# Token sums on VectorE behind the fourth plain tile, a fourth raw-weight buffer, and block results formed in place, in a chain of four transformer layers

## The chip, the cores and the metric

The kernel runs on one core of one Trainium2 chip. The metric is the device time of one execution, in microseconds (us). A core has five engines that run their own instruction queues in order: TensorE (PE) for matmuls, VectorE (DVE), ScalarE (ACT) and GpSimd (POOL) for elementwise work, and SyncE (SP), which here issues the DMA loads of the weights. Semaphores join them.

## The reference

The input is 512 tokens of 1024 features in float32. Two hybrid layers (retention, sparse and dilated attention, then an MLP) and a norm are followed by two layers with a mixer and a gated feed-forward part each. What the change touches is the MLP and the gated part, cut to this:

```python
# hybrid layer, twice: w_up is 1024 x 4096, w_down 4096 x 1024
h = rms_norm(x, mlp_norm_w)
x = x + jnp.square(jax.nn.relu(h @ w_up)) @ w_down

# second block, two layers: w_gate and w_up are 1024 x 2816, w_down 2816 x 1024
h = rmsnorm(x, ffn_pre_g[layer])
x = x + rmsnorm((jax.nn.silu(h @ w_gate) * (h @ w_up)) @ w_down, ffn_post_g[layer])
```

## The kernel before

**Layout.** Activations lie feature-major: x is eight tiles of 128 features by 512 tokens. Each float32 operand of a matmul is split into a high half (rounded to the matmul's type, on ACT) and a low half (the rest, on DVE or POOL), and a product is three matmuls (mm3, L318 to L323: high by high, high by low, low by high). A weight tile is loaded by SP into `raw` (three buffers, L255), its high half goes into `whi` (L268) and its low half into `wlo` (L269), three buffers each. A plain output tile is 8 x 3 matmuls of 512 columns.

**Pairs.** Most output tiles of the up and gate projections are made two at a time by `seven` (L402): two tiles by two halves of the tokens, each with two halves of the 1024 inputs, are a 2 x 2 block product, done with seven block products instead of eight (Winograd's form of Strassen's scheme). It needs sums of blocks of the weights and sums of blocks of the tokens. `pair_weights` (L374) loads the two raw tiles and forms a1 (a plain half), s12 and s34 (the weight sums, with four POOL operations, L393 to L397, in two buffers of the tag "sum", then split into `shi` and `slo`, L386 and L387) and a2. `token_sums` (L352) forms the token sums once a stage: for each of four feature blocks k, two scaled tiles on ACT (L359), four differences of 128 x 256 on POOL (L363 to L366, into a buffer of "sum"), a high half on ACT (L369) and a low half on DVE (L370).

**A pair's steps.** `seven` is a generator with three steps. The first runs products p1, p2 and p3 (12 matmuls of 256 columns each), copies p1 to r1 (L426) and adds it to p2 (r2, L427). The second runs p1 with the other plain half and p2 with s34; r3 is formed (L433) and one half of u (L434). The third runs p2 with a2 and p3 with s34 and forms the last halves (L438, L439); `post` then does the activation and the split (low half on POOL, L276). `pairs` runs steps one of this pair, three of the pair before, two of this pair, so two pairs are open at once. The tiles t and u come from the tag "t" (four buffers, `temp`, L235), from which `squared`, `tile` and `token_sums` take theirs too.

**Order.** A scheduler sets each engine's order when the kernel is built: it works through instructions by program order as they become ready in its own timing, and gives buffers of a tag to the takers in program order. `after` adds an edge that holds an instruction behind another one without a semaphore where both are on one engine. In the hybrid layers' `mlp` the program has three plain up tiles, `token_sums`, the fourth plain tile, then pairs (L991 to L994); there `post` and `squared` need two squares and the low half of a square on POOL for each tile. In the feed-forward `swiglu` it has three plain tiles, `token_sums`, and the fourth plain tile inside the second call of `product` (L1393 to L1396). `token_sums` runs four times in all, `seven` 64 times: 13 pairs in each hybrid MLP and 19 in each feed-forward stage.

## Time and profile before

| what | value |
|---|---|
| median of 3 runs | 2594.86 us (2590.73 to 2604.97) |
| the profiled execution's own time | 2592.7 us |
| its span | 2590.8 us |
| mean granted TensorE clock | 0.969 of full speed |
| busy share PE, DVE, ACT, POOL | 92%, 66%, 47%, 41% |
| DMA | 215.70 MB, 83 GB/s in the mean |

The span runs from the first to the last instruction of the profiled execution. Times of rows are microseconds from the span's start unless a row says ns. PEclk is the granted clock of PE as a share of its full 2.4 GHz. In a timeline row a bracket holds how long the engine stood idle before the instruction and what ended that wait.

### The profile page before, as it was taken

Reading aid. Unit: us, or ns where it says so; the run is one execution under the profiler, and the core shown is the slowest. Engines: PE = TensorE matmul, PEld = TensorE weight load, DVE = VectorE, ACT = ScalarE, POOL = GpSimd, SP = SyncE. Lnnn points to the kernel's source line nnn. Section 1 sums busy time; section 2 is a strip of 40 time slices with the busy share of each in tenths; the row PEclk is TensorE's granted clock in tenths of the full one; section 3 lists DMA queues with packets and bytes.
Section 4 is the critical chain, followed back from the end, with each engine's and each line's share of the span. In section 5 each row is a group of like instructions: output and inputs, shape, how many; then the busy total and the mean of one; then the engine's idle time right before and its main releaser. Section 6 shows DMA issues by size and latency. Waiting matters only on the chain.

```text
span 2590.8 us, 35121 instructions
## 1 busy us (share of the span) xinstructions
PE 2375.4 (92%) x13521; PEld 2040.4 (79%) x13521; DVE 1702.5 (66%) x2713; ACT 1216.1 (47%) x1945; POOL 1062.8 (41%) x755
## 2 busy tenths in 40 slices
PE   9899969999998997999998996999899987799997
PEld 7787868898877876888887874888886765788886
DVE  6978644554488875554558677756757675857655
ACT  5566553443365665343343564443434554444332
POOL 3464363342145644343312435543521543724531
PEclk9999989999999998999999998999999999899998
DMA  5211213333232211333332211333232321232322
GB/s 166 90 62 46 78 58 97 98 99 97 91 102 78 62 53 45 106 92 96 98 98 78 74 57 33 92 96 92 85 97 71 97 80 43 78 100 86 96 90 74
DMA packets 63848, 215.70 MB, mean 83 GB/s; under 512 B 7104, under 2 KB 7232, under 8 KB 63680
## 3 DMA queue, kind: packets, MB, share of 16 engines
q1 hardware_dynamic: 62064, 207.06, 26.1%
q0 software_dynamic: 1472, 6.29, 0.7%
q8 instruction: 106, 1.74, 0.3%
q14 instruction: 62, 0.51, 0.1%
q10 hardware_dynamic: 144, 0.11, 0.0%
HBM read 211.33 MB, written 2.10 MB: 82 GB/s over the span
## 4 chain that ended last, share of the span: by engine, by line
PE 63%; DVE 21%; ACT 5%; POOL 5%; issue 5%; DMA 1%; POOLq 0%; ACTq 0%; DVEq 0%; SPq 0%
PE mm L323 18%; PE mm L322 17%; PE mm L321 17%; DVE wlo L387 2%; PE st L322 2%; PE st L321 2%; PE st L323 2%; DVE slo L387 1%; DVE t L1367 1%; DVE x L1067 1%; ACT shi L386 1%; DMA raw<-in_w1up 1%; DVE score L739 1%; DVE t L1366 1%; PE st L307 1%
## 5 line engine op out<-in xcount | busy, mean ns | idle before, releaser
L268 ACT ACTIVATE whi<-raw 128x1024 fp32r<-128x1024 f32 (+2 forms) x286 | 277.8, 973 | 536.9 <-PE mm L322 361.3
L321 PE MATMUL mm<-xg,whi 128*128 128x512 f32 (+1 forms) x1280 | 448.1, 356 | 80.3 <-ACT r L426 34.2
L321 PE MATMUL mm<-act,whi 128*128 128x512 f32 x1160 | 456.8, 396 | 13.2 <-ACT act L275 8.3
L323 PE MATMUL mm<-xg,wlo 128*128 128x512 f32 (+1 forms) x1280 | 453.7, 355 | 11.1 <-DVE wlo L387 7.8
L322 PE MATMUL mm<-act,whi 128*128 128x512 f32 x1160 | 460.7, 397 | 0.8 <-POOL act L276 0.8
L323 PE MATMUL mm<-act,wlo 128*128 128x512 f32 x1160 | 461.1, 398 | 0.0
L322 PE MATMUL mm<-xg,whi 128*128 128x512 f32 (+1 forms) x1280 | 454.1, 355 | 0.2 <-DVE xg L315 0.2
L269 POOL TENSOR_TENSOR wlo<-raw,whi 128x1024 fp32r<-128x1024 f32 (+3 forms) x109 | 257.8, 2367 | 297.8 <-ACT whi L268 277.0
L321 PEld LDWEIGHTS mm<-xg,whi 128*128 128x128 f32 x1280 | 244.3, 192 | 121.3 <-ACT r L426 34.9
L387 DVE TENSOR_TENSOR slo<-sum,shi 128x1024 fp32r<-128x1024 f32 x128 | 176.2, 1377 | 229.9 <-ACT shi L386 220.4
L276 POOL TENSOR_TENSOR act<-t,act 128x512 fp32r<-128x512 f32 x108 | 160.5, 1495 | 346.3 <-ACT act L275 346.2
L323 PEld LDWEIGHTS mm<-xg,wlo 128*128 128x128 f32 x1280 | 244.6, 191 | 45.9 <-DVE wlo L387 8.8
L322 PEld LDWEIGHTS mm<-xg,whi 128*128 128x128 f32 x1280 | 245.2, 192 | 38.1 <-DVE xg L315 6.6
L321 PEld LDWEIGHTS mm<-act,whi 128*128 128x128 f32 x1160 | 221.0, 191 | 65.7 <-ACT act L275 11.1
L386 ACT ACTIVATE shi<-sum 128x1024 fp32r<-128x1024 f32 x128 | 135.8, 1061 | 272.3 <-POOL sum L394 169.5
L322 PEld LDWEIGHTS mm<-act,whi 128*128 128x128 f32 x1160 | 218.8, 189 | 52.8 <-DVE act L276 2.3
L323 PEld LDWEIGHTS mm<-act,wlo 128*128 128x128 f32 x1160 | 218.6, 188 | 47.8
L269 DVE TENSOR_TENSOR wlo<-raw,whi 128x1024 fp32r<-128x1024 f32 (+3 forms) x177 | 201.6, 1139 | 76.5 <-ACT whi L268 75.7
L393 POOL TENSOR_TENSOR sum<-raw 128x512 f32<-128x512 f32 x64 | 86.4, 1350 | 389.1 <-DMA raw<-in_w1up 179.4
L323 PE MATMUL mm<-tok,slo 128*128 128x256 f32 x512 | 150.6, 294 | 38.9 <-DVE slo L387 38.9
L387 DVE TENSOR_TENSOR wlo<-raw,whi 128x1024 fp32r<-128x1024 f32 (+1 forms) x128 | 153.6, 1202 | 9.3 <-ACT whi L386 9.3
L321 PE MATMUL mm<-tok,shi 128*128 128x256 f32 x512 | 148.6, 290 | 9.4 <-DVE r L427 6.8
(275 smaller groups left out, 5241.5 us busy)
## 6 DMA issues: line engine op xcount, KB each, us to landing
raw<-in_w1up SPq DMA_DIRECT2D x64, 512.0 KB, 3.6
raw<-in_w1down SPq DMA_DIRECT2D x64, 512.0 KB, 3.6
raw<-in_gate SPq DMA_DIRECT2D x44, 512.0 KB, 3.7
raw<-in_up SPq DMA_DIRECT2D x44, 512.0 KB, 3.6
raw<-in_w1fm SPq DMA_DIRECT2D x41, 512.0 KB, 3.5
raw<-in_down SPq DMA_DIRECT2D x48, 384.0 KB, 3.1
raw<-in_odin SPq DMA_DIRECT2D x16, 512.0 KB, 3.7
raw<-in_w1out SPq DMA_DIRECT2D x16, 384.0 KB, 3.0
```

The lines of the kernel that those rows point to most:

```text
L268: nc.scalar.activation(hi[:, sl], raw[:, sl], AF.Copy)
L269: (low or nc.gpsimd).tensor_sub(lo[:, sl], raw[:, sl], hi[:, sl].bitcast(F))
L276: (low or nc.vector).tensor_sub(lo, t, hi.bitcast(F))
L307: mm(ps, a[:, rows], b[hh][:, cols], start=True, stop=False, skip_group_check=True)
L321: mm(ps, w[0], a[0], start=first, stop=False, skip_group_check=True)
L322: mm(ps, w[0], a[1], start=False, stop=False, skip_group_check=True)
L323: self.last_mm = mm(ps, w[1], a[0], start=False, stop=last, skip_group_check=True)
L386: nc.scalar.activation(hi[:, :width], t, AF.Copy)
L387: nc.vector.tensor_sub(lo[:, :width], t, hi[:, :width].bitcast(F))
L393: nc.gpsimd.tensor_add(s1, a21, a22)
L739: nc.vector.match_replace(sl, m8, sl, TAKEN)
L1067: add = eng.tensor_add(self.x[c], self.x[c], m[c])
```

## The change

Five edits. (1) The `raw` tag gets four buffers, not three. (2) In `token_sums` the first scaled tile of a block comes from a tag "b1" of its own with one buffer, the second from "t" as before; the four differences go from POOL to DVE. (3) The high half of each token sum is ordered on ACT behind the last plain tile's weight high half that was issued before the call (`last_high`). (4) The fourth plain tile comes ahead of `token_sums` in both stages. (5) In `seven` the buffer r is 256 wide, not 768: r2 is formed in the half of t, and r3 in the half of u, in which the result will stand, so t and u are taken in the first step.

```diff
--- before.py
+++ after.py
@@ -185,7 +185,7 @@
         zero = self.cp.tile([128, 128], R, name="zero")
         nc.vector.memset(zero.bitcast(F), 0.0)
         self.keep_warm(14, of=zero)
-        self.early = [self.wp.tile([128, 1056], F, tag="raw", name=self.name("raw")) for _ in range(3)]
+        self.early = [self.wp.tile([128, 1056], F, tag="raw", name=self.name("raw"), bufs=4) for _ in range(3)]
         for c in range(8):
             nc.sync.dma_start(self.x[c], I["x"][c * 128:(c + 1) * 128, :])
             if c in (0, 3):
@@ -253,7 +253,7 @@
 
 
     def load(self, src, width):
-        raw = self.wp.tile([128, 1056], F, tag="raw", name=self.name("raw"))
+        raw = self.wp.tile([128, 1056], F, tag="raw", name=self.name("raw"), bufs=4)
         self.nc.sync.dma_start(raw[:, :width], src)
         return raw
 
@@ -265,7 +265,7 @@
         lo = self.wp.tile([128, 1056], R, tag="wlo", name=self.name("wlo"))
         for a in range(0, width, step):
             sl = slice(a, a + step)
-            nc.scalar.activation(hi[:, sl], raw[:, sl], AF.Copy)
+            self.last_high = nc.scalar.activation(hi[:, sl], raw[:, sl], AF.Copy)
             (low or nc.gpsimd).tensor_sub(lo[:, sl], raw[:, sl], hi[:, sl].bitcast(F))
         return hi, lo
 
@@ -352,21 +352,21 @@
     def token_sums(self, x, g):
 
 
-        nc, out = self.nc, []
+        nc, out, high = self.nc, [], self.last_high
         for k in range(4):
-            b = [self.temp() for _ in range(2)]
-            for i in range(2):
-                nc.scalar.activation(b[i], x[k + 4 * i], AF.Copy, scale=g(k + 4 * i))
-            (b11, b12), (b21, b22) = [(t[:, :256], t[:, 256:]) for t in b]
+            b1, b2 = self.temp("b1", 1), self.temp()
+            for i, b in enumerate((b1, b2)):
+                nc.scalar.activation(b, x[k + 4 * i], AF.Copy, scale=g(k + 4 * i))
+            (b11, b12), (b21, b22) = [(b[:, :256], b[:, 256:]) for b in (b1, b2)]
             f = self.get("sum", 2 * S)
             t1, t2, t3, t4 = [f[:, 256 * i:256 * i + 256] for i in range(4)]
-            nc.gpsimd.tensor_sub(t1, b12, b11)
-            nc.gpsimd.tensor_sub(t2, b22, t1)
-            nc.gpsimd.tensor_sub(t3, b22, b12)
-            nc.gpsimd.tensor_sub(t4, b21, t2)
+            nc.vector.tensor_sub(t1, b12, b11)
+            nc.vector.tensor_sub(t2, b22, t1)
+            nc.vector.tensor_sub(t3, b22, b12)
+            nc.vector.tensor_sub(t4, b21, t2)
             t = self.get("tok", 4 * S, R)
             hi, lo = t[:, :2 * S], t[:, 2 * S:]
-            nc.scalar.activation(hi, f, AF.Copy)
+            self.after(nc.scalar.activation(hi, f, AF.Copy), high)
             nc.vector.tensor_sub(lo, f, hi.bitcast(F))
             out.append((hi, lo))
         return out
@@ -418,25 +418,23 @@
                 self.mm3(ps, (w[0][:, sl], w[1][:, sl]), b(k), first and k == 0, k == 3)
 
         p1, p2, p3 = (t[:, :256] for t in (self.mm_tile(), self.mm_tile(), self.st_tile()))
-        r = self.get("r", 768)
-        r1, r2, r3 = (r[:, 256 * i:256 * i + 256] for i in range(3))
+        r, t, u = self.get("r", 256), self.temp(), self.temp()
         product(p1, a1, 0, plain(0, 0), True)
         product(p2, s12, 1, summed(1), True)
         product(p3, s12, 0, summed(0), True)
-        nc.scalar.activation(r1, p1, AF.Copy)
-        nc.vector.tensor_add(r2, p2, r1)
+        nc.scalar.activation(r, p1, AF.Copy)
+        nc.vector.tensor_add(t[:, half[1]], p2, r)
         yield
-        t, u = self.temp(), self.temp()
         product(p1, a1, 1, plain(1, 0), False)
         product(p2, s34, 0, summed(2), False)
         nc.scalar.activation(t[:, half[0]], p1, AF.Copy)
-        nc.vector.tensor_add(r3, p2, r1)
-        nc.vector.tensor_add(u[:, half[1]], p3, r3)
+        nc.vector.tensor_add(u[:, half[1]], p2, r)
+        nc.vector.tensor_add(u[:, half[1]], p3, u[:, half[1]])
         yield
         product(p2, a2, 0, summed(3), False)
         product(p3, s34, 1, plain(1, 1), False)
-        nc.vector.tensor_add(u[:, half[0]], p2, r1)
-        nc.vector.tensor_add(t[:, half[1]], p3, r2)
+        nc.vector.tensor_add(u[:, half[0]], p2, r)
+        nc.vector.tensor_add(t[:, half[1]], p3, t[:, half[1]])
         post(t, u)
         yield
 
@@ -989,8 +987,8 @@
                 next(left.pop())
 
         up(range(3))
+        up([3])
         tok = self.token_sums(x, lambda c: self.v("mlp_norm", 8 * l + c))
-        up([3])
         pairs([4, 6])
         for g in range(4):
             if g < 3:
@@ -1391,9 +1389,10 @@
                 nc.vector.tensor_add(m[j], m[j], ps)
 
         p = self.fm_tiles([plain("gate", 0), plain("up", 0), plain("gate", 1)], xg)
+        last = self.fm_tiles([plain("up", 1)], xg)[0]
         tok = self.token_sums(self.x, lambda c: self.v("ffn_pre", 8 * l + c))
         product(0, tile(p[0]), tile(p[1]))
-        product(1, tile(p[2]), tile(self.fm_tiles([plain("up", 1)], xg)[0]))
+        product(1, tile(p[2]), tile(last))
         pairs(range(2, 6))
         for g, n in enumerate((6, 6, 6, 4)):
             if g < 3:
```

## Rows read from the trace of the kernel before

**Rows 1.** The page's busy table: engine, busy us, share of the span, instructions.

```profile
PE 2375.4 (92%) x13521; PEld 2040.4 (79%) x13521; DVE 1702.5 (66%) x2713; ACT 1216.1 (47%) x1945; POOL 1062.8 (41%) x755
```

**Rows 2.** Busy time by stretch, inside the first wait: engines, granted clock, DMA share, GB/s.

```profile
342.00:352.00 10.00, 0.00 (x0) 0.00 (x0) 3.60 (x4) 5.63 (x8) 8.28 (x10) 0.50 0.00 0
```

**Rows 3.** PE's timeline (start, us, operation, idle before) and waits (total, times, longest).

```profile
352.57 0.58 PE L321 MATMUL mm<-xg,whi 128*128 128x256 f32 x1 [17.03 <-ACT r L426]
355.27 0.58 PE L321 MATMUL mm<-tok,shi 128*128 128x256 f32 x1 [0.20 <-ACT shi L386]
362.68 0.35 PE L321 MATMUL mm<-tok,shi 128*128 128x256 f32 x1 [2.52 <-DVE r L427]
...
1608.76 0.80 PE L321 MATMUL mm<-xg,whi 128*128 128x512 f32 x1 [16.02 <-ACT whi L268]
...
POOL sum L393 <- DMA raw<-in_w1up: 179.4, 19, 17.4
...
PE mm L323 <- DVE slo L387: 38.9, 26, 2.4
PE mm L321 <- ACT r L426: 34.2, 3, 17.0
PE mm L321 <- ACT whi L268: 32.6, 3, 16.0
```

**Rows 4.** Timelines of ACT and POOL in the first hybrid MLP, around the token sums.

```profile
350.67 1.06 ACT L369 ACTIVATE tok<-sum 128x1024 fp32r<-128x1024 f32 x1 [2.77 <-POOL sum L366]
...
352.15 0.36 ACT L426 ACTIVATE r<-mm 128x256 f32<-128x256 f32 x1
...
331.93 3.91 POOL L276 TENSOR_TENSOR act<-t,act 128x512 fp32r<-128x512 f32 x3
...
350.60 1.26 POOL L393 TENSOR_TENSOR sum<-raw 128x512 f32<-128x512 f32 x1
```

**Rows 5.** Durations by line: ns min/median/max, first and last start us, forms.

```profile
L359 ACT ACTIVATE t<-x,vec_sb x32: 705/707/726, 330.4 to 2201.0; 128x512 f32<-128x512 f32 x32
...
L366 POOL TENSOR_TENSOR sum<-t,sum x16: 716/722/727, 337.2 to 2205.4; 128x256 f32<-128x256 f32 x16
...
L370 DVE TENSOR_TENSOR tok<-sum,tok x16: 1215/1226/1449, 339.0 to 2207.2; 128x1024 fp32r<-128x1024 f32 x16
...
L433 DVE TENSOR_TENSOR r<-mm,r x64: 407/412/425, 369.0 to 2536.7; 128x256 f32<-128x256 f32 x64
```

**Rows 6.** Timeline of ACT in the first feed-forward stage, around the token sums.

```profile
1586.68 1.93 ACT L359 ACTIVATE t<-x,vec_sb 128x512 f32<-128x512 f32 x3
...
1604.76 1.06 ACT L369 ACTIVATE tok<-sum 128x1024 fp32r<-128x1024 f32 x1 [1.79 <-POOL sum L366]
...
1607.66 1.04 ACT L268 ACTIVATE whi<-raw 128x1024 fp32r<-128x1024 f32 x1
...
1620.14 0.38 ACT L426 ACTIVATE r<-mm 128x256 f32<-128x256 f32 x1 [0.60 <-PE mm L323]
```

**Rows 7.** Timelines of DVE and POOL ahead of that stage: one sum beside POOL's, one alone.

```profile
1581.56 1.80 DVE L1067 TENSOR_TENSOR x<-x,m 128x512 f32<-128x512 f32 x1
...
1584.82 0.68 DVE L1067 TENSOR_TENSOR x<-x,m 128x512 f32<-128x512 f32 x1
...
1581.52 1.29 POOL L498 TENSOR_TENSOR acc<-acc,t 128x512 f32<-128x512 f32 x1 [1.97 <-ACT t L492]
```

**Rows 8.** Timelines of ACT, DVE and POOL in a run of feed-forward pairs.

```profile
1720.76 1.06 ACT L386 ACTIVATE shi<-sum 128x1024 fp32r<-128x1024 f32 x1 [2.43 <-PE st L322]
...
1731.69 0.41 DVE L427 TENSOR_TENSOR r<-mm,r 128x256 f32<-128x256 f32 x1
...
1742.11 0.68 DVE L1353 TENSOR_TENSOR t<-t,t 128x512 f32<-128x512 f32 x1
...
1743.97 0.41 DVE L427 TENSOR_TENSOR r<-mm,r 128x256 f32<-128x256 f32 x1
...
1746.39 2.28 POOL L276 TENSOR_TENSOR act<-t,act 128x512 fp32r<-128x512 f32 x1
```

## The prediction

> **What bounds the kernel now.** I read the page's busy table first: PE is busy for 92% of the span [rows 1], so a time can only come down where PE stands still or runs at its lower clock. Next came PE's waits, longest first, and then PE's timeline around the longest of them [rows 3]. The reader is to see that two entries, of three waits each, hold 66.8 us together, and that their longest waits are 17.0 and 16.0 us. They lie at the four calls of token_sums. In the MLP of the hybrid layers PE stops at 335.54 (352.57 less 17.03) and first touches a token sum at 355.27; the second hybrid layer repeats it. In the feed-forward stages PE stops at 1592.74 (1608.76 less 16.02), and the other stage repeats that. In such a wait the granted clock falls to 0.50, the lower of its two levels [rows 2], and PE's first microseconds after it are at that level.
>
> Who holds PE is read from the other queues. In the hybrid stage PE waits for r L426, the copy of a finished block out of PSUM. It stands in ACT's queue behind the fourth token high half, which ends at 351.73; that one waited for POOL, which did three 1.3 us low halves of squared tiles (3.91 us) between the sixteen token differences and reached the first difference of the pair's weights only at 350.60 [rows 4]. So even a free ACT would have met s12, the first weight sum, at 354.16 or so. In the feed-forward stage PE waits for whi L268, the high half of the fourth plain tile's weights; its raw tile lay ready, but ACT did all four token high halves first and came to it at 1607.66 [rows 6].
>
> **The change, part by part.** The profiled execution took 2592.7 us (span 2590.8 and 1.9 around it); the median of the three runs is 2594.86. The sum is made against 2592.7.
>
> *Differences from POOL to VectorE.* POOL took 0.72 us for each [rows 5], 64 in all, 2.9 us per block. The trace has no 128x256 difference of SBUF operands on DVE. Its nearest row is the PSUM form at 0.41 us [rows 5]; twice that, 0.82, is the upper bound, from the row in which a DVE sum beside a POOL operation took 1.80 instead of 0.68 [rows 7] (that factor of 2.6 applies to one that starts just behind POOL; not each of four in a row can). A bound below 0.41 has no reason in any row. I take 0.41, since POOL has little else to do there. A block then costs DVE 4 x 0.41 + 1.23 (low half L370 [rows 5]) = 2.87 us, and ACT 2 x 0.71 + 1.06 = 2.48 us [rows 5, 6]. DVE sets the pace.
>
> *Hybrid stage, with the fourth plain tile ahead of the sums.* That tile's matmuls already lay ahead of the wait, so the move itself is worth nothing there; but its temporary now comes before those of the sums. The second scaled block takes a slot of "t" that a squared tile gives back when POOL has made its low half. Those low halves no longer stand between differences: the first can end near 332.4, the others 1.3 us apart [rows 4]. From there: scaled block 0.7, three differences 1.2 (the first needs only b1), high half 1.06, low half 1.23: 336.7. Three more blocks at 2.87: 345.3, and 0.7 for the fourth tile's evacuation on DVE: 346. The weight sums share the two buffers of "sum" with the token blocks, so s12 starts when the third block's low half is done, near 343: two POOL sums 2.6 and shi 1.06 put PE's first token matmul at 346.7 in place of 355.27, 8.6 us earlier. The second sum can start at 346 and its low half is there by 351, so the next step, held until 362.68 in the trace [rows 3], starts near 351.3: 11.4 us earlier. What is late after that in the trace is the next pair's second raw tile (below), with some 2 us of short waits and as much of lower clock; I count 2.6 of it. Together 14 us. Bounds: 8.6 (nothing but the first token matmul moves) and 18.
>
> *Feed-forward stage, with the fourth tile ahead and the high halves held behind its whi.* The ordering edge costs no wait of a semaphore, since both lie in ACT's queue; behind it stand the token high halves alone. The fourth tile can begin by 1592.7 at the latest, 16 us earlier, and keeps PE until about 1598. The token blocks start on ACT at 1586.68 [rows 6]. DVE then has 4 x 2.87 = 11.5 us of them, 1.2 us of the fourth tile's low half, 0.7 us of the small steps of the norm and, I estimate, 1 us of gaps: done at 1601, the third block at 1598.5. With 2.6 + 1.06 us for s12 the first token matmul is at 1602.2. Now it follows the evacuation at 1620.14 [rows 6]: 17.7 us earlier. Some of this is given back. In a run of feed-forward pairs one pair follows the other after 12.28 us (1731.69 to 1743.97 [rows 8]) of which PE waits 1.5 us for slo (38.9 us in 26 waits [rows 3]), since DVE's queue is late with it, and runs its next matmuls at the lower clock (0.7, my estimate). The first two pairs escape that today, since DVE and POOL work ahead while PE stands; afterwards they will not: 2 x 2.2 = 4.4 us. Left: 13 us. Bounds: 8 and 17.7.
>
> *Four raw buffers.* POOL waited 179.4 us for in_w1up [rows 3], nearly always off PE's path. A pair needs two raw tiles and the next pair's second one had no slot. With four, SP issues it a pair earlier, and no transfer shares an engine's queue but SP's own, where only later loads stand. Beyond the 2.6 us above I take 0. Bounds: a loss of 5 us, if earlier POOL sums meet DVE at worse places, and a gain of 10.
>
> *Block results in place.* Counts and shapes stay: five DVE sums and two ACT copies a pair. But the sum of L427 now writes t, so t and u are taken in a pair's first step, not its second, and DVE waits if no slot is free; behind it stand slo of the pair's second sum and the evacuations of the pair before. Slots go to the next taker in the order in which they come free: shi at 1720.76 takes the one that its own pair's first sum had left on PE [rows 8]. So t takes the slot of u of two pairs back, whose last reader ends at 1742.79, ahead of L427 at 1743.97 [rows 8]; cover 1.2 us. I take 0.
>
> Sum: 2 x 14 + 2 x 13 = 54; 2592.7 - 54 = 2538.7, called 2539.
>
> **The rivals.** *A, half the gain.* DVE's differences meet POOL's four squared low halves and its weight sums. At 1.12 us more (1.80 less 0.68 [rows 7]) for each of six meetings a site loses 6.7 us: 4 x 6.7 = 27, which gives 2566. For it: such stretches are found all over the feed-forward stages. Against it: POOL is nearly empty while the sums are made. The Trainium skill (SBUF — State Buffer, Who interferes with whom) has a rule that speaks against the move: a VectorE instruction with both inputs in SBUF and a GpSimd instruction that reads SBUF exclude each other, and the later one waits for the whole of the other. Rows 7 agree; the differences fall under it, the PSUM sums from which I took 0.41 do not.
>
> *B, slower.* t must wait for the slot of t of two pairs back, which POOL's low half gives free at 1748.67 (1746.39 + 2.28 [rows 8]), 4.7 us after L427's time. Then slo and the next pair's queue slip by some 3 us. It decides from 54 / 64 pairs = 0.85 us a pair. The pairs with two others just before them are 22 in the feed-forward stages, 66 us at 3; the other 42 at 0.5 give 21: 2538.7 + 87 = 2626. For it: the cover is 1.2 us. Against it: the slot order above, and in the hybrid stage slots come free within about a microsecond of the need.
>
> *C, no change.* The scheduler starts the token blocks no earlier, or s12, which needs the shared "sum" buffers, takes the place of the old wait: 2593.
>
> *D, more.* Earlier sums also take DVE's contention away, and most of the 38.9 us waited for slo goes: 2500.
>
> **How the numbers follow.** Forecast 0.65, A 0.17, B 0.07, C 0.06, D 0.05. The forecast's own bounds: 2 x 18 + 2 x 17.7 + 10 = 81 us and 2 x 8.6 + 2 x 8 - 5 = 28 us, thus 2512 to 2565. With A's further side the range is 2512 to 2578; B, C and D are outside. A measurement of this kernel tells about 0.5% (13 us) from no change. Faster by more: forecast, A and D, 0.87; within: C and a little of B, 0.07; slower by more: 0.06.
>
> **What would show each step.** Right: PE's waits of 16 to 17 us are gone from all four sites, with 3 to 11 us left, put down to shi L386 (POOL sum before it); whi of the fourth plain tile ahead of every token high half on ACT; differences on DVE of 0.41 us; the first token matmul near 347 and 1602; POOL's waits for in_w1up shorter. Wrong, by step: differences of 0.8 us or more (A); L427 waiting for POOL act L276, and more waits for slo in runs of pairs (B); PE still idle until about 355 or 1619 (C). The prediction falls if the sites gain but the long runs of pairs, which hold most of the time, lose more than 0.5 us a pair.

## The result and the profile after

The changed kernel takes 2529.86 us in the median of four runs (2529.12 to 2536.21), the kernel before in runs beside it 2596.91 (2590.73 to 2604.97). The ratio is 0.9745, with a 95% interval of 0.9713 to 0.9777: faster, by about 66 us. The forecast was 2539, with 2512 to 2578 as its range. The sum came out near; its two large terms did not, and most of what follows is about that.

The page's busy table of the kernel after answers to [rows 1] (engine, busy us, share of the span, instructions):

```profile
PE 2359.3 (93%) x13521; PEld 2028.6 (80%) x13521; DVE 1736.7 (69%) x2777; ACT 1216.2 (48%) x1945; POOL 1019.9 (40%) x691
```

PE's work is the same 13521 matmuls, and they take 16.1 us less than before, since the mean granted clock rose from 0.969 to 0.978. DVE took over 64 instructions from POOL. Of the 62.8 us between the two profiled spans (2590.8 and 2528.0) the busy time thus gives 16.1 us, and the rest is time in which PE no longer stands still.

Waits of the kernel after (who waited for whom: us in total, times, longest us), to be laid beside [rows 3]:

```profile
POOL sum L393 <- DMA raw<-in_w1up: 129.5, 15, 10.8
...
POOL sum L393 <- DMA raw<-in_up: 84.3, 11, 8.5
...
PE mm L321 <- ACT shi L386: 29.5, 4, 11.3
...
PE mm L323 <- DVE slo L387: 29.2, 24, 1.4
...
PE mm L321 <- ACT r L425: 17.1, 2, 8.5
```

The two waits of 17.0 and 16.0 us are gone. What is left of them at the four sites is 8.5 us for r (in the hybrid stages alone), and 3.5 and 11.3 us for shi. POOL waits 50 us less for in_w1up, and for in_up 84.3 us where it was 169.8. The 38.9 us of waits for slo have become 29.2.

To see where the time went, one mark a pair is enough: the first matmul of its third step on PE (tok by whi). 64 such marks stand in each trace. Between the same marks of two kernels the difference of time is what the kernel gained or lost in that stretch. Two of them, the first and the last pair of the first feed-forward stage, in the kernel before (in the kernel after they stand at 1592.40 and 1891.18):

```profile
1629.97 0.28 PE L321 MATMUL mm<-tok,whi 128*128 128x256 f32 x1
...
1937.74 0.28 PE L321 MATMUL mm<-tok,whi 128*128 128x256 f32 x1
```

The run between them took 307.77 us before and 298.78 after: 8.99 us gained in a stretch in which no token sum is made. The table has these differences for all four stages, for the kernel after and for the experiments below, each against the profiled execution of the kernel before. "Site" is the gain between the last pair of the stage before and the first pair of this one (it holds the mixers too, which differ by some us from one execution to another), "run" is the gain from the first to the last pair.

| kernel | hybrid 1: site, run | hybrid 2: site, run | feed-forward 1: site, run | feed-forward 2: site, run | all runs |
|---|---|---|---|---|---|
| forecast | 14, 0 | 14, 0 | 13, 0 | 13, 0 | 0 |
| after | 9.9, 6.2 | 9.2, 6.4 | 5.9, 9.0 | 5.7, 10.9 | 32.5 |
| e1_raw4 | 0.4, 7.4 | -4.5, 7.5 | 1.3, 8.8 | 1.5, 10.9 | 34.6 |
| e3_tokens | 13.9, -7.2 | 10.1, -6.7 | 3.6, -1.1 | 4.2, 2.0 | -12.9 |
| e4_after_raw3 | 10.4, -5.8 | 13.3, -7.5 | 4.5, 0.3 | 5.0, 1.8 | -11.3 |
| e5_pool | 2.1, 6.8 | 1.5, 7.0 | 0.9, 9.0 | 1.2, 10.9 | 33.7 |
| e7_blk | 7.0, 10.4 | 6.3, 10.5 | 8.3, 8.8 | 8.6, 11.0 | 40.8 |
| e8_order | 8.3, 6.9 | 2.7, 7.1 | 3.0, 9.1 | 2.0, 11.0 | 34.1 |
| e9_nohold | 5.0, 6.2 | 4.1, 6.4 | 6.0, 9.0 | 4.9, 11.0 | 32.6 |
| e12_late | 6.5, 4.2 | 5.6, 4.5 | 4.3, 0.5 | 4.7, 3.8 | 13.0 |

In the kernel after, the four sites hold 30.7 us (forecast 54) and the runs 32.5 (forecast 0). The row of e9_nohold shows how far the mixers move a site: it has the order of the kernel after on every engine, the same runs, and up to 5 us less at a site. Counted from the first matmul of a stage's plain tiles to its first pair, without the mixers, the four sites gain 9.7, 9.5, 5.1 and 4.9 us in the kernel after (29.1 in all) and 9.7, 9.6, 5.1 and 3.4 in e9_nohold. Where the text below says "without the mixers", this count is meant.

**The site in the first hybrid layer.** Timeline (start, us, engine, line, idle before and what ended it), to be laid beside [rows 4]:

```profile
334.74 0.70 ACT L359 ACTIVATE t<-x,vec_sb 128x512 f32<-128x512 f32 x1
...
336.92 0.41 DVE L366 TENSOR_TENSOR sum<-t,sum 128x256 f32<-128x256 f32 x1
...
345.23 1.39 POOL L393 TENSOR_TENSOR sum<-raw 128x512 f32<-128x512 f32 x1 [6.77 <-DVE tok L370]
...
345.40 1.50 DVE L365 TENSOR_TENSOR sum<-t,b 128x256 f32<-128x256 f32 x1
...
346.82 1.48 DVE L366 TENSOR_TENSOR sum<-t,sum 128x256 f32<-128x256 f32 x1
...
348.33 1.06 ACT L369 ACTIVATE tok<-sum 128x1024 fp32r<-128x1024 f32 x1 [4.45 <-DVE sum L366]
...
350.39 0.58 PE L321 MATMUL mm<-tok,shi 128*128 128x256 f32 x1 [3.53 <-ACT shi L386]
```

A difference on DVE takes 0.41 us, as counted, and 58 of the 64 take 0.41 to 0.43. The two that lie beside the weight sums on POOL take 1.50 and 1.48, and the fourth token high half waits 4.45 us for the second of them. With it shi, which stands behind it, and PE come late. The first second-half scaled tile starts only at 334.74, behind the pair's whi, which itself waited for PE. The first token matmul is at 350.39: 4.9 us earlier than in [rows 3], not 8.6.

**The site in the first feed-forward stage.** This timeline runs 31.6 us ahead of the one before (the mark of the last hybrid pair moved from 1314.98 to 1283.35), so 1559 answers to 1590.6 of [rows 6]:

```profile
1556.85 1.06 ACT L268 ACTIVATE whi<-raw 128x1024 fp32r<-128x1024 f32 x1 [1.36 <-PE mm L322]
...
1559.00 1.06 ACT L369 ACTIVATE tok<-sum 128x1024 fp32r<-128x1024 f32 x1 [1.08 <-DVE sum L366]
...
1568.56 0.68 DVE L1356 TENSOR_TENSOR t<-mm,rb 128x512 f32<-128x512 f32 x1
...
1569.16 3.45 DVE L370 TENSOR_TENSOR tok<-sum,tok 128x1024 fp32r<-128x1024 f32 x2
...
1571.56 2.18 POOL L393 TENSOR_TENSOR sum<-raw 128x512 f32<-128x512 f32 x1 [1.16 <-DVE tok L370]
...
1573.82 2.12 POOL L394 TENSOR_TENSOR sum<-sum,raw 128x512 f32<-128x512 f32 x1
...
1577.08 0.58 PE L321 MATMUL mm<-tok,shi 128*128 128x256 f32 x1 [11.29 <-ACT shi L386]
...
1586.51 0.39 PE L321 MATMUL mm<-tok,shi 128*128 128x256 f32 x1 [1.64 <-DVE t L426]
```

The order is as forecast: whi of the fourth plain tile ahead of the first token high half, and PE does that tile with one short wait (0.55 us for wlo L269). Then PE waits 11.29 us for shi. Windows of 4 us (the columns are those of [rows 2]: PE, PEld, DVE, ACT, POOL, granted clock, DMA share, GB/s) show who is busy in that wait:

```profile
1568.00:1572.00 4.00, 0.00 (x0) 0.00 (x0) 4.00 (x5) 3.98 (x6) 1.71 (x2) 0.51 0.00 0
...
1572.00:1576.00 4.00, 0.00 (x0) 0.00 (x0) 4.00 (x4) 0.03 (x1) 3.92 (x3) 0.50 0.00 0
```

DVE is busy all the time, from 1560 on: three evacuations of plain tiles (L1356, 0.68 us) and a product (L1351, 0.69 us) stand between the token blocks, and the last two low halves behind them take 3.45 us together in place of 2 x 1.23. The weight sums on POOL take 2.18 and 2.12 us instead of 1.3, beside DVE. The granted clock falls to 0.51 and 0.50 there, its lower level, as in [rows 2], and PE's first matmuls behind the wait still run at it:

```profile
1577.08:1581.70 4.62, 4.62 (x21) 4.62 (x22) 2.36 (x2) 1.83 (x3) 2.93 (x3) 0.50 0.20 43
```

In the kernel before the fourth plain tile ran in that time, and the first token matmul found the clock at 1.00.

### The profile page after: what moved, and what is told of

Its sections match the earlier page's. It is cut to its first block, busy times and chain, and to the rows that moved or that the text cites. A ratio compares the mean times of both kernels' runs of the same rounds, so it can differ in the third digit from the quotient of the medians.

```text
span 2528.0 us, 35109 instructions
## 1 busy us (share of the span) xinstructions
PE 2359.3 (93%) x13521; PEld 2028.6 (80%) x13521; DVE 1736.7 (69%) x2777; ACT 1216.2 (48%) x1945; POOL 1019.9 (40%) x691
## 4 chain that ended last, share of the span: by engine, by line
PE 69%; DVE 20%; ACT 4%; issue 4%; POOL 2%; DMA 0%; POOLq 0%; ACTq 0%; DVEq 0%
PE mm L323 19%; PE mm L322 19%; PE mm L321 19%; PE st L322 2%; PE st L321 2%; DVE wlo L387 2%; PE st L323 2%; DVE slo L387 1%; DVE x L1065 1%; DVE t L1365 1%; PE st L307 1%; DVE score L737 1%; DVE m L736 1%; PE st L308 1%; PE st L632 1%
## 5 line engine op out<-in xcount | busy, mean ns | idle before, releaser
L269 POOL TENSOR_TENSOR wlo<-raw,whi 128x1024 fp32r<-128x1024 f32 (+3 forms) x109 | 257.8, 2367 | 295.3 <-ACT whi L268 285.0
L321 PEld LDWEIGHTS mm<-xg,whi 128*128 128x128 f32 x1280 | 244.4, 192 | 71.2 <-ACT xg L314 19.9
L276 POOL TENSOR_TENSOR act<-t,act 128x512 fp32r<-128x512 f32 x108 | 145.2, 1355 | 387.6 <-ACT act L275 387.6
L321 PEld LDWEIGHTS mm<-act,whi 128*128 128x128 f32 x1160 | 220.6, 191 | 62.8 <-ACT act L275 11.1
L386 ACT ACTIVATE shi<-sum 128x1024 fp32r<-128x1024 f32 x128 | 135.8, 1061 | 256.1 <-POOL sum L394 119.1
L269 DVE TENSOR_TENSOR wlo<-raw,whi 128x1024 fp32r<-128x1024 f32 (+3 forms) x177 | 200.2, 1131 | 68.5 <-ACT whi L268 67.8
L393 POOL TENSOR_TENSOR sum<-raw 128x512 f32<-128x512 f32 x64 | 96.7, 1510 | 310.8 <-DMA raw<-in_w1up 129.5
L387 DVE TENSOR_TENSOR wlo<-raw,whi 128x1024 fp32r<-128x1024 f32 (+1 forms) x128 | 179.2, 1403 | 14.9 <-ACT whi L386 13.1
L323 PE MATMUL mm<-tok,slo 128*128 128x256 f32 x512 | 149.1, 291 | 29.2 <-DVE slo L387 29.2
```

What stands on the lines that cost most here:

```text
L269: (low or nc.gpsimd).tensor_sub(lo[:, sl], raw[:, sl], hi[:, sl].bitcast(F))
L276: (low or nc.vector).tensor_sub(lo, t, hi.bitcast(F))
L321: mm(ps, w[0], a[0], start=first, stop=False, skip_group_check=True)
L323: self.last_mm = mm(ps, w[1], a[0], start=False, stop=last, skip_group_check=True)
L386: nc.scalar.activation(hi[:, :width], t, AF.Copy)
L387: nc.vector.tensor_sub(lo[:, :width], t, hi[:, :width].bitcast(F))
```

## The experiments

### The parts alone

e1_raw4 is the kernel before with four raw buffers (and with r3 formed in u and r 512 wide, which makes the room in the on-chip memory that the fourth buffer takes):

```diff
-        raw = self.wp.tile([128, 1056], F, tag="raw", name=self.name("raw"))
+        raw = self.wp.tile([128, 1056], F, tag="raw", name=self.name("raw"), bufs=4)
...
-        r = self.get("r", 768)
+        r = self.get("r", 512)
...
-        nc.vector.tensor_add(r3, p2, r1)
-        nc.vector.tensor_add(u[:, half[1]], p3, r3)
+        nc.vector.tensor_add(u[:, half[1]], p2, r1)
+        nc.vector.tensor_add(u[:, half[1]], p3, u[:, half[1]])
```

> The kernel before with four raw buffers alone (the third value of r stands in u, formed where it was formed before, since there is no room for it otherwise; t and u are taken in the second step as before). Theory, the fourth raw buffer made the gains in the runs of pairs: 25 to 40 us faster than before, with waits of 17 and 16 us still there at the four sites of the token sums. Rival, the results in place made them: within 10 us of before.

Measured: 2556.82 us (2554.09 to 2559.36), ratio 0.9859 (0.9838 to 0.9881), 37 us faster than the 2593.78 of the kernel before beside it. The long waits at the sites are untouched:

```profile
PE mm L321 <- ACT r L426: 34.0, 2, 17.0
...
PE mm L321 <- ACT whi L268: 32.8, 4, 16.0
```

So the buffer alone brings more than half of the whole gain, and all of it in the runs (34.6 us in the table), where the forecast had put nothing.

e2_inplace is the kernel before with the block results in place, alone:

```diff
-        r = self.get("r", 768)
+        r, t, u = self.get("r", 256), self.temp(), self.temp()
...
-        nc.vector.tensor_add(r2, p2, r1)
+        nc.vector.tensor_add(t[:, half[1]], p2, r)
...
-        nc.vector.tensor_add(r3, p2, r1)
-        nc.vector.tensor_add(u[:, half[1]], p3, r3)
+        nc.vector.tensor_add(u[:, half[1]], p2, r)
+        nc.vector.tensor_add(u[:, half[1]], p3, u[:, half[1]])
```

> The kernel before with the block results formed in place alone (t and u taken in a pair's first step, r 256 wide, three raw buffers). Theory, the fourth raw buffer: within 8 us of before. Rival, in place: 25 to 35 us faster. Second rival, B of the prediction: L427 waits for a slot of t and the kernel is slower by 10 us or more.

Measured: 2594.01 us, ratio 1.0002 (0.999 to 1.0014). It is worth nothing, as counted. The wait that rival B was built on does exist, though not where B put it, as the waits of this kernel show:

```profile
DVE t L426 <- POOL act L276: 8.5, 10, 0.9
```

Ten waits of 0.85 us, all in the hybrid stages and none in the feed-forward ones; the kernel after has the same ten, and in the time they cost nothing.

e3_tokens is the kernel before with the token part alone (differences on DVE, the fourth plain tile first, the high halves held):

```diff
-            nc.gpsimd.tensor_sub(t1, b12, b11)
+            nc.vector.tensor_sub(t1, b12, b11)
...
-            nc.scalar.activation(hi, f, AF.Copy)
+            self.after(nc.scalar.activation(hi, f, AF.Copy), high)
...
+        last = self.fm_tiles([plain("up", 1)], xg)[0]
-        product(1, tile(p[2]), tile(self.fm_tiles([plain("up", 1)], xg)[0]))
+        product(1, tile(p[2]), tile(last))
```

> The kernel before with the token part alone: differences on VectorE, the fourth plain tile ahead, the high halves held (three raw buffers, r as before). From the changed kernel's trace the four sites gained 9.3, 9.0, 5.5 and 5.7 us by the first pair's end: 25 to 32 us faster than before. If the sites need the fourth raw buffer too, 10 to 20 us.

e4_after_raw3 is the kernel after with three raw buffers:

```diff
-        raw = self.wp.tile([128, 1056], F, tag="raw", name=self.name("raw"), bufs=4)
+        raw = self.wp.tile([128, 1056], F, tag="raw", name=self.name("raw"))
```

> The changed kernel with three raw buffers. Theory, the fourth raw buffer made the gains in the runs: it loses 25 to 40 us of the 67 and stays 25 to 35 us faster than before. Rival, in place: it stays within 8 us of the changed kernel.

Measured: e3_tokens 2573.18 us, ratio 0.9919 (0.9897 to 0.994); e4_after_raw3 2573.03, ratio 0.9923 (0.9899 to 0.9947). The two agree, so the token part without the buffer brings 21 us, not the 54 less 5.2 that the sum had for it. In the table the hybrid sites of these two kernels gain 10 to 14 us, and 6 to 7.5 are lost again in the run, nearly all at one pair, the second: its mark moves by -6.8 us in both kernels (-0.6 in the kernel after). The larger part of this is the mark itself: with three buffers PE begins the first pair's third step ahead of the second pair's token products, so the first mark comes some 4 us early and gains nothing for what follows. The timelines of e4_after_raw3 and of the kernel after show this and the rest:

```profile
353.82 0.58 PE L321 MATMUL mm<-tok,shi 128*128 128x256 f32 x1 [3.51 <-ACT shi L386]
...
360.57 1.29 POOL L393 TENSOR_TENSOR sum<-raw 128x512 f32<-128x512 f32 x1 [2.98 <-DVE t L426]
...
362.80 0.39 PE L321 MATMUL mm<-tok,whi 128*128 128x256 f32 x1 [0.36 <-DVE t L431]
...
365.91 0.58 PE L321 MATMUL mm<-tok,shi 128*128 128x256 f32 x1 [2.25 <-ACT shi L386]
...
367.37 2.23 POOL L393 TENSOR_TENSOR sum<-raw 128x512 f32<-128x512 f32 x1 [1.26 <-DMA raw<-in_w1up]
```

```profile
354.69 1.28 POOL L393 TENSOR_TENSOR sum<-raw 128x512 f32<-128x512 f32 x1
...
361.77 1.30 POOL L393 TENSOR_TENSOR sum<-raw 128x512 f32<-128x512 f32 x1
```

Counted from the first token matmul, the first pair's mark comes after 8.98 us with three buffers (362.80) and after 12.95 with four (363.34 less 350.39). The weight sum of the second pair starts after 6.75 us with three and after 4.30 with four (354.69 less 350.39), and that of the third pair after 13.55 and 11.38. With three, SP issues the second pair's tile only at 356.38 (the row of 360.57 names t L426 as what came last), the third pair's sum waits for its tile by name, and PE waits 2.25 us for shi. Up to the second pair's mark, without the mixers, the hybrid sites gain 9.1 us with four buffers in both layers and 6.8 to 7.4 with three. This is the "next pair's second raw tile" of the prediction, counted there at 2.6 us a site; it is worth 1.6 to 2.3.

### What the fourth buffer does in the feed-forward runs

Here no long wait of PE for a tile is to be found, before or after. The two kernels differ in when POOL makes the first weight sums of a pair. A pair of the first feed-forward stage in the kernel before, then the same pair in the kernel after (the first operation of a weight sum on POOL; an slo on DVE; the matmul that waits for the slo behind that one in DVE's queue):

```profile
1720.25 1.29 POOL L393 TENSOR_TENSOR sum<-raw 128x512 f32<-128x512 f32 x1 [3.78 <-DMA raw<-in_up]
...
1721.85 2.15 DVE L387 TENSOR_TENSOR slo<-sum,shi 128x1024 fp32r<-128x1024 f32 x1 [1.97 <-ACT shi L386]
...
1729.95 0.39 PE L323 MATMUL mm<-tok,slo 128*128 128x256 f32 x1 [1.75 <-DVE slo L387]
```

```profile
1675.92 1.62 POOL L393 TENSOR_TENSOR sum<-raw 128x512 f32<-128x512 f32 x1 [3.44 <-DVE slo L387]
...
1681.72 1.23 DVE L387 TENSOR_TENSOR slo<-sum,shi 128x1024 fp32r<-128x1024 f32 x1 [1.97 <-ACT shi L386]
...
1688.89 0.39 PE L323 MATMUL mm<-tok,slo 128*128 128x256 f32 x1 [0.84 <-DVE slo L387]
```

Before, the sum waits for its raw tile, and its second half L394, at 1721.62, runs while that slo (1721.85) is made: that one takes 2.15 us instead of 1.2. All that follows in DVE's queue is late by as much, the slo of the next weight sum too, and PE waits 1.75 us for it. After, the raw tile is there, the sum starts 5.80 us ahead of slo instead of 1.60, both halves are done before it, slo takes 1.23 us, and PE waits 0.84 us: 0.92 us less in DVE's queue and 0.91 us less on PE.

In the hybrid runs it is other waits. In the first of them PE waits for the low half of a pair's plain weights, in the kernel before (its waits from 373.19 to 635.84) and then after (363.34 to 619.80):

```profile
PE mm L323 <- DVE wlo L387: 3.9, 2, 2.0
```

```profile
PE mm L323 <- DVE wlo L387: 0.5, 1, 0.5
```

Of the 6.2 us gained there 3.9 are waits and 2.3 are faster matmuls.

To test whether the time at which POOL makes the sums is the cause, e12_late keeps the four buffers and makes half of the first weight sum twice:

```diff
-        nc.gpsimd.tensor_add(s1, a21, a22)
+        nc.gpsimd.tensor_add(s1[:, :256], a21[:, :256], a22[:, :256])
+        full = nc.gpsimd.tensor_add(s1, a21, a22)
...
-        nc.gpsimd.tensor_sub(s3, a11, a21)
+        self.after(nc.gpsimd.tensor_sub(s3, a11, a21), full)
```

> The changed kernel with one more operation on POOL in each of the 64 pairs: the first 256 columns of the first weight sum are made twice, by a 128x256 sum just ahead of L393 into the same buffer. All four raw buffers stay, the raw tiles land as early as in the changed kernel, and the order on every engine is the same but for the 64 sums; only the pair's weight sums end some 0.7 to 0.9 us later. Theory (the fourth buffer pays because the weight sums start earlier and so no longer run beside the low half of the pair before, whose lateness in DVE's queue PE then waits for): much of the fourth buffer's gain goes, 2550 to 2570 us, the waits of PE for slo L387 rise above 40 us, and the difference lies in the runs of pairs, 0.3 to 0.6 us a pair. Rival (it pays because tiles are there when a pair begins, and POOL, busy 40% of the span, has the slack for 46 us more): under 8 us slower than the changed kernel, 2530 to 2538.

Measured: 2558.38 us (2554.31 to 2559.66), ratio 0.9861 (0.9838 to 0.9883). 28.5 us of the gain are gone, though the four buffers are there. The rival is out. The first pair of the same stage in the kernel after, then in this one:

```profile
1593.62 1.32 DVE L387 TENSOR_TENSOR slo<-sum,shi 128x1024 fp32r<-128x1024 f32 x1 [1.18 <-ACT shi L386]
...
1600.89 0.39 PE L323 MATMUL mm<-tok,slo 128*128 128x256 f32 x1 [0.93 <-DVE slo L387]
```

```profile
1603.18 2.44 POOL L393 TENSOR_TENSOR sum<-raw 128x256 f32<-128x256 f32 x2
...
1605.97 2.11 DVE L387 TENSOR_TENSOR slo<-sum,shi 128x1024 fp32r<-128x1024 f32 x1 [1.20 <-ACT shi L386]
...
1614.02 0.39 PE L323 MATMUL mm<-tok,slo 128*128 128x256 f32 x1 [1.72 <-DVE slo L387]
```

L394, at 1605.70, now falls on slo (2.11 us), and PE waits 1.72 us. In the table the runs of the feed-forward stages lose 15.6 of their 19.9 us, those of the hybrid stages only 3.8 of 12.6; the sites lose 3.6 us without the mixers, and the rest lies in parts that have no pairs. So in the feed-forward stages the time at which POOL makes the sums decides most of the gain; in the hybrid ones most of it outlives the delay.

The theory's path is not borne out as a whole. All waits for slo together rose to 33.0 us, not above 40, and not every pair is like the first: of the eleven waits in the first feed-forward stage six are now 1.72 to 1.88 us and five 0.68 to 0.89, where the kernel after has 0.84 to 1.42. The pair shown above, at 1688.89, waits 0.84 us in both. The larger part of the loss is the clock, which the stretch from the first to the last pair of the first feed-forward stage shows. Before, after and e12_late (columns as above; PE busy is the first number behind the length):

```profile
1629.97:1937.74 307.77, 287.98 (x1934) 265.77 (x1933) 202.63 (x254) 123.58 (x174) 129.65 (x85) 0.99 0.30 91
```

```profile
1592.40:1891.18 298.78, 284.91 (x1935) 262.89 (x1933) 203.53 (x255) 124.07 (x174) 129.49 (x86) 1.00 0.31 95
```

```profile
1604.74:1912.05 307.31, 292.37 (x1934) 270.37 (x1933) 202.39 (x255) 124.10 (x174) 148.75 (x102) 0.97 0.30 93
```

What PE is not busy is 19.8, 13.9 and 14.9 us, and the eleven waits of PE for slo in each of these stretches sum to 19.8, 13.9 and 14.9 as well: in this run PE waits for slo and for nothing else. The gain of 8.99 us is 5.9 us of these waits and 3.1 of faster matmuls. Of e12_late's loss of 8.5 us only 1.1 are waits and 7.5 are matmuls at a lower clock (0.97 in the mean). DVE is busy for 202 to 204 us in all three: the added sums on POOL (19 us more) don't make DVE's work longer in all, they change which of its operations are stretched.

In this stretch the granted clock falls to its lower level, 0.50, twice in the kernel before, never in the kernel after and five times in e12_late, and each fall costs some 1.5 us. Every fall comes with a wait for slo of 1.72 us or more, but not every such wait has one: two of nine in the kernel before, five of six in e12_late; the kernel after has no such wait. A wait of 1.72 us in e12_late and one of 1.73 us in the kernel before, each with the 4 us behind it:

```profile
1612.00:1616.00 4.00, 2.28 (x16) 2.07 (x15) 4.00 (x8) 1.53 (x3) 1.82 (x2) 0.89 0.44 131
...
1616.00:1620.00 4.00, 4.00 (x26) 4.00 (x26) 1.15 (x3) 1.28 (x2) 3.39 (x3) 0.68 0.46 131
```

```profile
1739.00:1743.00 4.00, 2.27 (x18) 2.07 (x18) 4.00 (x6) 0.81 (x2) 0.90 (x1) 1.00 0.44 128
...
1743.00:1747.00 4.00, 4.00 (x36) 4.00 (x36) 2.16 (x5) 2.31 (x4) 3.17 (x3) 1.00 0.45 134
```

In the one the clock falls (0.68 in the mean of the window) and PE gets 26 matmuls done in 4 us, in the other it stays at 1.00 and PE does 36. Waits and busy time in the two windows with the wait are alike (2.28 and 2.27 us busy). Why one is followed by a fall and the other isn't, these runs don't tell.

The scheduler also changes its order on ACT, DVE and POOL when the kernel before is given four buffers: shi and slo of a group's first pair come earlier in the queues. In e12_late the order on every engine is that of the kernel after, but for the added sums; so what it loses is a matter of time alone. How much of the gain that it keeps, most of it in the hybrid stages, is order and how much the presence of the tiles stays open.

### The parts of the token sums

e5_pool is the kernel after with the differences on POOL:

```diff
-            nc.vector.tensor_sub(t1, b12, b11)
-            nc.vector.tensor_sub(t2, b22, t1)
-            nc.vector.tensor_sub(t3, b22, b12)
-            nc.vector.tensor_sub(t4, b21, t2)
+            nc.gpsimd.tensor_sub(t1, b12, b11)
+            nc.gpsimd.tensor_sub(t2, b22, t1)
+            nc.gpsimd.tensor_sub(t3, b22, b12)
+            nc.gpsimd.tensor_sub(t4, b21, t2)
```

> The changed kernel with the four differences of a token block on POOL again; order, hold, raw buffers and results in place as in the changed kernel. Theory, the move to VectorE is worth part of the sites' gain: the last token high half ended 2.3 us (hybrid) and 3.3 us (feed-forward) earlier than in the kernel before, counted from the norm ahead, and POOL is then free for the weight sums: 12 to 20 us slower than the changed kernel. Rival, VectorE is the full engine at the feed-forward sites and the move gives nothing: within 6 us of it, or faster.

Measured: 2552.89 us, ratio 0.9835 (0.9821 to 0.985); 23 us slower than the kernel after, more than the theory's 12 to 20; the rival is out. Without the mixers each site loses 4.1 to 6.6 us, 21.5 together; the runs gain 1.2. In the first feed-forward stage the last difference on POOL ends at 1593.50, the weight sums stand behind it in POOL's queue, and PE, which had already waited 7.59 us for the plain half whi L386, waits for shi:

```profile
1592.77 0.73 POOL L366 TENSOR_TENSOR sum<-t,sum 128x256 f32<-128x256 f32 x1
...
1598.11 0.58 PE L321 MATMUL mm<-tok,shi 128*128 128x256 f32 x1 [3.88 <-ACT shi L386]
```

e8_order is the kernel after with the fourth plain tile behind the token sums and no hold:

```diff
-            self.after(nc.scalar.activation(hi, f, AF.Copy), high)
+            nc.scalar.activation(hi, f, AF.Copy)
...
-        up([3])
         tok = self.token_sums(x, lambda c: self.v("mlp_norm", 8 * l + c))
+        up([3])
...
-        last = self.fm_tiles([plain("up", 1)], xg)[0]
-        product(1, tile(p[2]), tile(last))
+        product(1, tile(p[2]), tile(self.fm_tiles([plain("up", 1)], xg)[0]))
```

> The changed kernel with the program order of the kernel before (the fourth plain tile behind the token sums) and without the hold of the high halves; differences on VectorE, four raw buffers, results in place. Theory, the order gives most of the gain at the feed-forward sites and the earlier temporaries some at the hybrid ones: 12 to 30 us slower than the changed kernel, with a wait for whi L268 of 8 us or more at the feed-forward sites. Rival, the move to VectorE did it: within 6 us.

Measured: 2540.90 us, ratio 0.9784 (0.9766 to 0.9801); 11 us slower than the kernel after, just short of the theory's 12 and beyond the rival's 6; 9.6 us of it are at the sites without the mixers, and the runs lose nothing. With the differences on DVE the token high halves are done earlier, so whi of the fourth tile behind them holds PE for 5.5 us, where the theory had 8 or more and [rows 3] had 16.0. The move of the differences and the move of the tile overlap in what they give.

e9_nohold leaves out the hold alone:

```diff
-            self.after(nc.scalar.activation(hi, f, AF.Copy), high)
+            nc.scalar.activation(hi, f, AF.Copy)
```

> The changed kernel without the edge that holds the token high halves behind the fourth tile's whi on ACT; all else as changed. Theory, program order alone keeps whi ahead: within 6 us of the changed kernel. Rival, the edge is what the feed-forward sites need: 8 to 16 us slower, with a high half ahead of whi L268 on ACT.

Measured: 2532.60 us, ratio 0.9762 (0.974 to 0.9784). The interval takes in the kernel after. The order on every engine is the same with and without the hold, so the hold does nothing here.

### Towards a faster site

e7_blk puts the token differences into buffers of the tag "act" and so takes them out of the way of the weight sums:

```diff
-            f = self.get("sum", 2 * S)
+            f = self.get("act", 2 * S)
```

> The changed kernel with the differences formed in buffers of the tag act, so that they no longer share the two buffers of the tag sum with the weight sums. Theory, the shared buffers hold s12 back until the third token block is split, and PE waits for that (shi L386, 11.3 us at a feed-forward site, 3.5 at a hybrid one): s12 comes as soon as its raw tiles are there, and the four sites gain 15 to 25 us together. Rival, the weight sums then run on POOL beside VectorE's differences, which take 1.5 us instead of 0.41 beside POOL: within 8 us of the changed kernel.

Measured: 2525.10 us (2521.07 to 2529.18), ratio 0.973 (0.9712 to 0.9747): 5 us below the kernel after in the median, though the two intervals overlap. PE's wait for shi in the feed-forward stages falls from 11.29 to 5.61 us. Against the kernel after the sites there gain 2.4 and 2.3 us without the mixers. In the hybrid stages PE's order at the first pairs differs, and the first mark says little; up to the second pair's mark they gain 2.5 us each. That is some 10 us at the four sites, not the theory's 15 to 25, and the time lies in the rival's range.

e10_evac also holds the plain tiles' evacuations behind the last token low half:

```diff
+            self.last_tok = nc.vector.tensor_sub(lo, f, hi.bitcast(F))
...
+            mul = nc.vector.tensor_mul(t, ps, rb)
+            if held:
+                self.after(mul, self.last_tok)
...
-        product(0, tile(p[0]), tile(p[1]))
-        product(1, tile(p[2]), tile(last))
+        product(0, tile(p[0], True), tile(p[1], True))
+        product(1, tile(p[2], True), tile(last, True))
```

> The changed kernel with the token differences in buffers of the tag act (as in e7_blk, 2525 us) and, in the two feed-forward stages, the evacuations of the four plain tiles held on DVE behind the last token low half. Theory (three evacuations of 0.68 us and what follows them stand in the full DVE queue between the token blocks and delay the first token matmul): the token sums are done 2 to 3 us earlier, the first token matmul comes 2 to 3 us earlier in each feed-forward stage, 2519 to 2523 us. Rival (the held tiles keep their PSUM buffers, which the first pair's products need, and POOL and ACT get their work later): what the token sums gain is lost at the first pair, 2525 to 2535.

e11_poollow puts two of the four token low halves of a feed-forward stage on POOL:

```diff
-            nc.vector.tensor_sub(lo, f, hi.bitcast(F))
+            (nc.gpsimd if k < pool else nc.vector).tensor_sub(lo, f, hi.bitcast(F))
...
-        tok = self.token_sums(self.x, lambda c: self.v("ffn_pre", 8 * l + c))
+        tok = self.token_sums(self.x, lambda c: self.v("ffn_pre", 8 * l + c), 2)
```

> The changed kernel with the token differences in buffers of the tag act (as in e7_blk, 2525 us) and, in the two feed-forward stages, the low halves of the token blocks 0 and 1 (L370, 128x1024) on POOL. Theory (DVE, full for 16 us, is the bound of the feed-forward site): 2.5 us come off DVE's queue there, the first token matmul comes 2 to 3 us earlier in each, 2519 to 2523 us. Rival (DVE and POOL stand in each other's way, so that what leaves one queue lengthens the other's operations, and POOL's low halves delay the weight sums behind them): 2525 to 2535.

Measured: e10_evac 2526.52 us (2517.94 to 2529.46), ratio 0.9735 (0.9702 to 0.9768); e11_poollow 2529.77 (2520.14 to 2532.96), ratio 0.9747 (0.9717 to 0.9777). Neither can be told from e7_blk. In e10_evac the scheduler filled the room with the first pair's own low halves on DVE and turned its products round on PE, so the first token matmul came 3.2 us earlier but the last token low half 1.7 us later, PE then waits 3.3 us for an slo, and the site gains 0.3 us: it doesn't tell the theories apart. In e11_poollow the first token matmul is 1.6 us earlier, counted from the first scaled tile (38.67 us, 40.27 in e7_blk), but the next step waits:

```profile
1561.91 6.86 POOL L370 TENSOR_TENSOR tok<-act,tok 128x1024 fp32r<-128x1024 f32 x1 [3.41 <-ACT tok L369]
...
1572.71 0.58 PE L323 MATMUL mm<-tok,slo 128*128 128x256 f32 x1 [5.13 <-DVE slo L387]
```

The other low half on POOL took 2.41 us; this one, beside a busy DVE, took 6.86 (spans on POOL are rough), and PE waits 5.13 us for an slo. The rival holds.

## Why the prediction was right, and where its steps were not

- **What bounds the kernel.** Right for the four waits, too narrow for the rest. The second largest thing to gain, the 38.9 us of waits for slo in [rows 3] with the clock that falls behind some of them, was read as something that the change leaves alone.
- **Differences at 0.41 us on DVE.** Right for 58 of 64. The six others took 0.96 to 1.50. [rows 7] and the rule of the Trainium skill (SBUF — State Buffer, Who interferes with whom), that a VectorE instruction with both inputs in SBUF and a GpSimd instruction that reads SBUF exclude each other, agree with the trace: 1.50 and 1.48 us beside POOL's sums. Both sides pay: POOL's sums took 2.18 us beside DVE.
- **Hybrid site, 14 us.** Its cause and its releasers were right (shi behind a POOL sum, 3.5 us; r 8.5 us), its size was 9.5 to 9.7 without the mixers, of which the second raw tile, counted at 2.6, is 1.6 to 2.3. The terms that failed: "three more blocks at 2.87" left out that two of the differences meet the weight sums (2 x 1.08 us), and the first block's second scaled tile, put at 332.4, came at 334.74 behind whi.
- **Feed-forward site, 13 us.** The order was right and PE did the fourth tile in the old wait. The first token matmul came 11.2 us earlier than before (1577.08 plus 31.6 is 1608.7, against 1619.94), not 17.7. DVE's queue was counted with 1 us of gaps and without the plain tiles' evacuations: four operations, 2.7 us, stand in it before the last low halves, which were 1 us slower in addition. The weight sums took 4.4 us instead of 2.6. What was to be given back behind it, 4.4 us, is 5.3 in the trace (11.2 less 5.9), near in size by luck: it was to come from the slo waits of the first two pairs with 0.7 us of lower clock behind each, but those waits are 0.93 and 1.40 us with the clock at 1.00. It comes ahead of the first mark: 4.62 us at the clock's lower level behind the long wait, a wait of 1.64 us for t L426, and ten more matmuls between the first token matmul and the mark.
- **Rival A** named a part of the loss: contention at the sites. It was priced at 27 us in all, and the sites fell short by 23 to 25; but in the two sites shown contention accounts for 2.2 us (two differences) and 2.8 us (low halves 1.0, weight sums 1.8), some 10 us in all four. All of it was then outweighed by something that the rival didn't know of.
- **Four raw buffers.** The 2.6 us inside each hybrid site were about right. The step "beyond the 2.6 us above I take 0", with a bound of 10, failed: the runs gained 32.5 us. The buffer alone gave 37 us, and taking it from the kernel after cost 43. The step asked only whether PE waits for a tile, and found the waits of POOL "nearly always off PE's path". They were not: they set when POOL's sums run, these decide which DVE operation is stretched, and DVE's queue decides when PE gets slo. In the first feed-forward run this path shows as 5.9 us of shorter waits and 3.1 us of clock; e12_late shows that the time of the sums matters, but brings few of the waits back, so the path is argued where it is more than the pairs shown. The sign of the risk was seen ("earlier POOL sums meet DVE at worse places") and its size and direction were not.
- **In place: 0.** Right. The slot order that was argued holds in the feed-forward stages; rival B's wait is there ten times in the hybrid ones, at 0.85 us, with nothing behind it that PE waits for.
- **Rival D** ("earlier sums also take DVE's contention away") described what the buffer does, and had 0.05. About a quarter of the waits for slo went, not most.

So the total was near because two errors of opposite sign met: 23 to 25 us too many at the sites, 32.5 too few in the runs. The warning at the end of the prediction, that the long runs of pairs decide, was the right place to look, with the sign turned round.

## What to carry to other kernels

When a buffer is added in a stage that repeats many times, don't only ask whether the bound engine waits for it: ask when its consumers on side engines will run, and beside what. One mark a repeat on the bound engine, compared between two traces, shows whether a gain lies at the places that were changed or is spread over the loop; but where the engine's order around a mark differs between the two, the mark moves without any gain, as at the first hybrid pair with three buffers. And when work is moved to an engine for a short stretch, count everything that stands in its queue in that stretch, the neighbours' evacuations too.

## What the runs showed of the hardware that was not expected

- One operation of some 1 us more on POOL a pair cost 19.5 us in the runs of 64 pairs (e12_late), and of the 8.5 us in the run looked at seven eighths came as a lower clock of PE rather than as waits.
- Two waits of equal length, 1.72 and 1.73 us, with equal work around them, were followed by 4 us with a granted clock of 0.68 in the mean in one kernel and of 1.00 in the other.
- A 128x1024 difference on POOL took 2.41 us at one place and 6.86 us at another, beside a DVE that was never idle; the 512-wide sums on POOL take 2.2 instead of 1.3 us there.
